# The first stage of a two-layer hybrid network: memory keys and values ahead of the input norm

## The chip, the cores and the metric

One Trainium2 chip, one core of it. The metric is the device time of one execution in microseconds (us). A core has a matrix engine (TensorE, PE in the profile, with its weight loads shown as PEld), a vector engine (VectorE, DVE), a scalar engine (ScalarE, ACT), a general engine (GpSimd, POOL) and a queue engine (SyncE, SP) that here issues every DMA. Each engine works through its own list of instructions in order; semaphores make one wait for another.

## The reference

Two layers (one "even", one "odd") on 1024 tokens of width 1024, with a memory of 256 rows. Both layers read keys and values of the same normed memory, each through its own weights.

```
mem_n = rmsnorm(mem, mem_norm_g)                       # 256 x 1024
even_layer: u = rmsnorm(h, g); za, rq, rk, rv, xq, gate = split_cols(u @ w_in, EVEN_SPLITS)
            a = pool_mixer(za, ...); r = retention(rq, rk, rv); m = mem_attention(xq, mem_n, w_mem_kv)
            h + (concat([a, r, m]) * silu(gate)) @ w_out
odd_layer:  the same frame, with a sparse attention in place of pool_mixer and retention
mem_attention: mk, mv = split(mem_n @ w_mem_kv); softmax(xq mk^T / sqrt(128)) mv, 4 heads
```

## The kernel before

Everything is kept transposed: features lie on the partitions, tokens in the free dimension, in two halves of 512 tokens. Each matrix product of full precision is made of three products: an operand is split into a rounded part (written by ACT, names ending in h) and the rest (a subtraction by DVE, names ending in l), and `mm3` (L76 to L79) multiplies h by h, h by l and l by h. So a weight tile goes DMA into `wr` (or `wm` after the change), then ACT writes `wh`, then DVE writes `wl`, then PE can use it.

The program starts with a head stage of some 64 us (pool `mk0`):

- The eight tiles `xs` of the first half of x are loaded; ACT squares each (`sqx`), and PE sums each square over the partitions by `square_sum` (L141): four products with one column for each tile, 32 in all. The memory's eight tiles are squared and summed likewise (`sqm`, two for each tile, 16 in all). Each of these fp32 products is two instructions on PE.
- From the sums comes 1/rms: `rstd_col` scales on DVE (`rs`), and POOL raises to the power -1/2 (`rr` for x, `rrkm` for the memory). `spread` makes a diagonal of it (`dg`, DVE), multiplies it by ones on PE (`ps_t<-dg,ones`), and ACT copies the row (`rb` for x, `mrb` for the memory).
- `make_u` scales the eight `xs` by `rb` on DVE (L454) and splits them into `uh` and `ul`. The first projection of the even layer, `ps_mm<-uh,wh` with the weights `ev_za`, needs them.
- `mem_kv` (L293) scales and splits the memory into `mu0` to `mu3`, makes the keys of four heads (weights `ev_mk`, products of 256 columns, 24 for each head, called K0 to K3 below) and the values (weights `ev_mv` in four quarters, 48 products of 512 columns, called V). K0 to K3 are multiplied by `mrb` into `mkx` and stored to DRAM (`evmkd`), V is scaled into `mvx` and stored (`evmvd`).

All weights go through `wr`, two buffers of 128x1024, and through four pairs `wh`, `wl`. The memory's raw tiles come through `wr` too. Behind the head stage, the even layer's two halves follow; each loads the stored keys and values (`load_mkv4`: tiles `mkr`, `mvr`) and splits them. The odd layer calls `mem_kv` a second time, between its first pairs of projections (`proj_pair`, a Strassen product with sums of weights by POOL).

The code is written in one order, and a scheduler of the language then sets each engine's order by its own estimate of when things are ready. So every change to the code can move instructions elsewhere too.

Of the kernel before, what the change touches and what calls it, by code (L numbers as in the profile page):

```python
# [9 lines left out]
F32 = mybir.dt.float32  # L10
# [29 lines left out]
def net(tc, a, out, dbg=None):  # L40
# [22 lines left out]
    def bank(tag, shape=(128, HT)):  # L63
        if tag not in banks:
            tag = ALIAS[tag]
        return cur["ps"].tile(list(shape), F32, name="ps_" + tag, tag=tag, bufs=banks[tag])
# [68 lines left out]
            pe.matmul(ss[:, t:t + 1], acc[:, t * 128:(t + 1) * 128], ones[:, 0:1], start=True, stop=True)  # L135
        return rstd_col(ss, nt, keep)

    def square_sum(ss, sq, nt, k):

        for t in range(nt):  # L140
            pe.matmul(ss[:, t:t + 1], sq[:, t * 128:(t + 1) * 128], ones[:, 0:1],  # L141
                      start=k == 0 and t == 0, stop=k == 7, skip_group_check=True)

    def rstd_col(ss, nt, keep=None):
        rs = sm.tile([128, 4], F32, name="rs")
        dve.tensor_scalar(rs[:, :nt], ss[:, :nt], 1.0 / D, EPS, OP.mult, OP.add)
# [1 line left out]
        pool.tensor_tensor(rr[:, :nt], rs[:, :nt], mhalf[:, :nt], OP.pow)  # L148
        return rr

    def spread(rr, n, raw=False, r=None):
        nt = n // 128
        rb = bank("t")
        dg = tmp.tile([128, nt, 128], F32, name="dg", tag="uf", bufs=2)
        for t in range(nt):
            dve.tensor_scalar(dg[:, t], ident, rr[:, t:t + 1], None, OP.mult)
            if raw:
                pe.matmul(rb[:, t * 128:(t + 1) * 128], ones, dg[:, t], start=True, stop=True)
        if raw:
            return rb  # L160
        pe.matmul(rb[:, :n], ones, dg.rearrange("p a b -> p (a b)"), start=True, stop=True)
        if r is None:
            r = cur["late"].tile([128, n], F32, name="rb", tag="rb")
        act.copy(r, rb[:, :n])
        return r
# [124 lines left out]

    memst = {}

    def mem_kv(pre, slots, mrb, raw=None):  # L293


        u = []
        first = not memst
        for k in range(8):
            if raw is not None:
                r = raw[k // 4]  # L300
            elif k % 4 == 0:
                r = wraw(a["memT"][k:k + 4].rearrange("k p m -> p k m"))
            x = r[:, (k % 4) * NMEM:(k % 4 + 1) * NMEM]
            s = slots[k // 2][k % 2]
            uh, ul = s[:, :NMEM], s[:, NMEM:]
            act.activation(uh, x, AF.Copy, scale=gains[:, 3, k:k + 1])
            dve.scalar_tensor_tensor(ul, x, gains[:, 3, k:k + 1], uh.bitcast(F32), OP.mult, OP.subtract)
            if first:
                if k == 0:
                    ss = bank("t")  # L310
                sq = tm2.tile([128, NMEM], F32, name="sqm", tag="th", bufs=2)
                act.activation(sq, x, AF.Square)
                square_sum(ss, sq, 2, k)
            u.append((uh, ul))
        yield
        kd = [dr.tile([128, NMEM], F32, name=f"{pre}mkd{h}") for h in range(4)]
        vd = [dr.tile([128, HT], F32, name=f"{pre}mvd{m}") for m in range(2)]
        mkv[pre] = kd, vd
        for h in range(4):
            w = wload(a[pre + "_mk"][h])  # L320
            o = bank("s")
            gemm(o[:, :NMEM], w, u)
            if first and h == 0:
                memst["rr"] = rstd_col(ss, 2, "m")
            if h == 0:
                rb = spread(memst["rr"], NMEM, r=mrb)
            t = tmp.tile([128, HT], F32, name="mkx", tag="uf", bufs=2)
            dve.tensor_tensor(t[:, :NMEM], o[:, :NMEM], rb, OP.mult)
            sp.dma_start(kd[h], t[:, :NMEM])
        yield  # L330
        o2 = [bank("s"), bank("s")]
        for c in range(4):
            w = wload(a[pre + "_mv"][c])
            for kk in range(2):
                k = 2 * c + kk
                for m in range(2):
                    mm3(o2[m], u[k][0][:, m * 128:(m + 1) * 128], u[k][1][:, m * 128:(m + 1) * 128],
                        w[kk][0], w[kk][1], k == 0, k == 7)
        for m in range(2):
            t = tmp.tile([128, HT], F32, name="mvx", tag="uf", bufs=2)  # L340
            act.activation(t, o2[m], AF.Copy, scale=memst["rr"][:, m:m + 1])
            sp.dma_start(vd[m], t)
        yield

    def load_mkv(kv, h, p_, bufs):
# [90 lines left out]
    evx = ExitStack()  # L436
    tm2 = evx.enter_context(tc.tile_pool(name="tm2", bufs=1, reuse_waits="tile"))

    def make_u(srcs, n, gi, pool_, tag, rr=None, xs=None):
        def load(k):  # L440
            x = up.tile([128, n], F32, name="x", tag="x", bufs=4)
            sp.dma_start(x, srcs[k])
            return x

        if rr is None:
            acc = tm2.tile([128, n], F32, name="acc", tag="acc")
            for k in range(8):
                add_square(acc, load(k), n, k == 0)
            rr = rstd_of(acc, n)
        rb = spread(rr, n, r=tm2.tile([128, n], F32, name="rb", tag="rb"))  # L450
        u = []
        for k in range(8):
            uf = xs[k] if xs else tmp.tile([128, n], F32, name="uf", tag="uf", bufs=2)
            dve.scalar_tensor_tensor(uf, xs[k] if xs else load(k), gains[:, gi, k:k + 1], rb, OP.mult, OP.mult)  # L454
            uh = pool_.tile([128, n], F32R, name="uh", tag=tag, bufs=16)
            ul = pool_.tile([128, n], F32R, name="ul", tag=tag, bufs=16)
            split(uh, ul, uf)
            u.append((uh, ul))
        return u

    def load_mkv4(kv, p_):
        mk = p_.tile([128, 4, 2, NMEM], F32R, name="mk", tag="mk")
        mv = p_.tile([128, 2, 2, HT], F32R, name="mv", tag="mv")
        for h in range(4):
            t = p_.tile([128, NMEM], F32, name="mkr", tag="mkx", bufs=1)
            sp.dma_start(t, kv[0][h])
            split(mk[:, h, 0], mk[:, h, 1], t)
        for m in range(2):
            t = p_.tile([128, HT], F32, name="mvr", tag="mkx", bufs=1)
            sp.dma_start(t, kv[1][m])  # L470
            split(mv[:, m, 0], mv[:, m, 1], t)
        return mk, mv
# [53 lines left out]
            pass  # L526

    sp.dma_start(ident, a["ident"])
    with tc.tile_pool(name="mk0", bufs=1, reuse_waits="tile") as mp_:
        xs = [mp_.tile([128, HT], F32, name=f"xs{k}") for k in range(8)]  # L530
        ss = bank("t")
        for k in range(8):
            sp.dma_start(xs[k], a["xT"][k][:, :HT])
            sq = tm2.tile([128, HT], F32, name="sqx", tag="t2", bufs=2)
            act.activation(sq, xs[k], AF.Square)
            square_sum(ss, sq, 4, k)
        mrb = mp_.tile([128, NMEM + 24], F32, name="mrb")[:, :NMEM]
        slots = [[mp_.tile([128, HT], F32R, name=f"mu{k}{x}") for x in "hl"] for k in range(4)]
        mem = mem_kv("ev", slots, mrb)
        u = make_u(None, HT, 0, up, "u", rstd_col(ss, 4), xs)  # L540
        drain(mem)

    rh = []
# [1 line left out]
    if True:  # L545
# [11 lines left out]
        for hf in range(2):  # L557
# [80 lines left out]
            with ExitStack() as pc:  # L638
                pp = pc.enter_context(tc.tile_pool(name="pp", bufs=1, reuse_waits="tile"))
                mp_ = pc.enter_context(tc.tile_pool(name="mx", bufs=1, reuse_waits="tile"))  # L640

                def mem_head(h):
                    s1 = gate_s1(wload(a["ev_gate"][12 + h]), u, ep)
                    o = mem_att_w(wload(a["ev_xq"][h]), u, mk, mv, h, mp_)
                    y = make_yt(ep, o, s1, 0.5)
                    ys[12 + h] = split_y(ep, y, 16)

                pooled = pool_in(0)
                mk, mv = load_mkv4(mkv["ev"], mp_)
                mem_head(0)  # L650
                pool_out(0, pooled)
                mem_head(1)
                pool_gate(0, 1, 2)
                pooled = pool_in(1)
                mem_head(2)
                pool_out(1, pooled)
                mem_head(3)
                pool_gate(3)

            with tc.tile_pool(name="rp", bufs=1, reuse_waits="tile") as rp:  # L660
# [408 lines left out]
    with tc.tile_pool(name="mk1", bufs=1, reuse_waits="tile") as mp_:  # L1069
        raw = [mp_.tile([128, 4 * NMEM], F32, name=f"mraw{j}") for j in range(2)]  # L1070
        for j in range(2):
            sp.dma_start(raw[j].rearrange("p (k m) -> p k m", k=4), a["memT"][4 * j:4 * j + 4].rearrange("k p m -> p k m"))
        mrb = mp_.tile([128, NMEM], F32, name="mrb1")
        slots = [[mp_.tile([128, HT], F32R, name=f"mv{k}{x}") for x in "hl"] for k in range(4)]
        mem = mem_kv("od", slots, mrb, raw)
        for nm, i in (("kc", 0), ("vc", 0), ("q", 0)):
            proj_pair(nm, i)
            next(mem)
    rel_tables()
    proj_pair("q", 2)  # L1080
    compress()
# [375 lines left out]
```

## Time and profile before

| | us |
|---|---|
| median of 3 runs | 2005.99 (2005.44 to 2006.42) |
| profiled execution, device time | 2006.08 |
| its span, first to last instruction | 2004.30 |
| outside the span | 1.78 |

The profiled execution is within 0.1 us of the median. Times in the trace count from the span's start. A busy PE means an instruction was in it; whether PE worked at full clock is read from the granted clock and from the pitch of its products.

### The profile page before, as it was taken

How to read it: one execution, taken by the hardware profiler on the slowest of the kernel's cores; microseconds unless marked ns; L12 is line 12 of the kernel's file. 1: busy time of each engine (PE TensorE's matmuls, PEld its weight loads, DVE VectorE, ACT ScalarE, POOL GpSimd, SP SyncE). 2: the span in 40 equal slices, each digit the busy share in tenths (PEclk: the TensorE clock that was granted, in tenths of full speed). 3: DMA queues.
4: the chain of work that ended last, by engine and by line, in shares of the span. 5: the costliest groups of instructions: out<-in, count | busy, mean ns of one | idle time of the engine just before them, and what ended most of it. 6: DMA issues, size and time to landing. Idle time of an engine off the chain costs nothing.

```text
span 2004.3 us, 28802 instructions
## 1 busy us (share of the span) xinstructions
PE 1939.9 (97%) x9898; PEld 1629.3 (81%) x9898; DVE 1269.6 (63%) x2739; ACT 941.8 (47%) x1869; POOL 572.9 (29%) x601
## 2 busy tenths in 40 slices
PE   7999999999999999999999999997999999999997
PEld 6888888888888878787878788886888888888885
DVE  4666455665646564944549855765756677867674
ACT  4545332444432243522222434544756677667674
POOL 0120110011211000314537543333343444433422
PEclk9999999999999999998999999998999999999998
DMA  5524234442322444557646433438464532251412
GB/s 164 164 83 136 90 105 137 145 159 85 93 88 95 144 152 163 166 187 221 207 143 197 137 120 130 134 101 272 149 189 127 160 104 63 69 159 42 122 32 95
DMA packets 127959, 267.07 MB, mean 133 GB/s; under 512 B 15512, under 2 KB 32676, under 8 KB 127780
## 3 DMA queue, kind: packets, MB, share of 16 engines
q1 hardware_dynamic: 127812, 265.24, 41.5%
q8 instruction: 78, 1.28, 0.3%
q14 instruction: 69, 0.56, 0.1%
HBM read 206.44 MB, written 61.09 MB: 133 GB/s over the span
## 4 chain that ended last, share of the span: by engine, by line
PE 84%; DVE 6%; DMA 4%; issue 2%; POOL 2%; ACT 1%; SPq 0%; DVEq 0%; POOLq 0%; ACTq 0%
PE ps_mm L79 13%; PE ps_mm L77 13%; PE ps_mm L78 13%; PE ps_t L120 6%; PE ps_s L77 3%; PE ps_s L78 3%; PE ps_s L79 3%; PE ps_a L77 3%; PE ps_a L78 3%; PE ps_a L79 3%; PE ps_o L84 2%; PE ps_o L82 2%; PE ps_o L83 2%; PE ps_b L79 2%; PE ps_b L78 2%
## 5 line engine op out<-in xcount | busy, mean ns | idle before, releaser
L70 ACT CAST wh<-wr 128x512 fp32r<-128x512 f32 (+1 forms) x395 | 242.4, 618 | 467.9 <-PE ps_mm L78 301.2
L71 DVE TENSOR_TENSOR wl<-wr,wh 128x512 fp32r<-128x512 f32 (+2 forms) x295 | 220.1, 750 | 178.7 <-ACT wh L70 172.2
L77 PE MATMUL ps_mm<-uh,wh 128*128 128x512 f32 x640 | 252.4, 394 | 0.0
L79 PE MATMUL ps_mm<-uh,wl 128*128 128x512 f32 x640 | 251.8, 393 | 0.0
L78 PE MATMUL ps_mm<-ul,wh 128*128 128x512 f32 x640 | 251.6, 393 | 0.0
L77 PE MATMUL ps_mm<-yh,wh 128*128 128x512 f32 x512 | 204.0, 404 | 5.1 <-ACT wh L70 3.5
L79 PE MATMUL ps_mm<-yh,wl 128*128 128x512 f32 x512 | 204.0, 400 | 2.2 <-DVE wl L71 1.4
L78 PE MATMUL ps_mm<-yl,wh 128*128 128x512 f32 x512 | 205.1, 401 | 0.0
L71 POOL TENSOR_TENSOR wl<-wr,wh 128x512 fp32r<-128x512 f32 x100 | 134.6, 1348 | 204.6 <-ACT wh L70 152.9
L71 DVE TENSOR_TENSOR apl<-ps_t,aph 128x512 fp32r<-128x512 f32 x204 | 136.1, 671 | 44.0 <-ACT aph L70 34.4
L70 ACT CAST aph<-ps_t 128x512 fp32r<-128x512 f32 x204 | 115.0, 568 | 83.0 <-PE ps_o L83 42.5
L1225 POOL TENSOR_TENSOR Pw<-Pw,arc 128x640 f32<-128x640 f32 (+2 forms) x96 | 95.9, 999 | 157.4 <-DVE arc L1221 87.8
L79 PEld LDWEIGHTS ps_mm<-uh,wl 128*128 128x128 f32 x640 | 120.2, 188 | 24.6 <-DVE wl L71 0.3
L78 PEld LDWEIGHTS ps_mm<-ul,wh 128*128 128x128 f32 x640 | 120.3, 188 | 23.8
L77 PEld LDWEIGHTS ps_mm<-uh,wh 128*128 128x128 f32 x640 | 120.3, 188 | 23.8
L77 PEld LDWEIGHTS ps_mm<-yh,wh 128*128 128x128 f32 x512 | 96.4, 190 | 26.3 <-ACT wh L70 5.9
L79 PEld LDWEIGHTS ps_mm<-yh,wl 128*128 128x128 f32 x512 | 97.1, 190 | 22.3 <-DVE wl L71 2.5
L70 ACT CAST wh<-ws 128x512 fp32r<-128x512 f32 x88 | 53.9, 619 | 129.5 <-POOL ws L231 44.3
L78 PEld LDWEIGHTS ps_mm<-yl,wh 128*128 128x128 f32 x512 | 97.3, 190 | 19.2 <-issue 0.8
L71 DVE TENSOR_TENSOR wl<-ws,wh 128x512 fp32r<-128x512 f32 x88 | 77.6, 888 | 52.2 <-ACT wh L70 49.2
L1217 ACT ACTIVATE Ps<-Ps,anm 128x512 f32<-128x512 f32 (+3 forms) x96 | 74.6, 777 | 25.8 <-DVE anm L1214 25.4
L1227 ACT ACTIVATE Ps<-Ps,arc 128x512 f32<-128x512 f32 (+3 forms) x96 | 74.7, 778 | 19.9 <-DVE arc L1221 18.8
(997 smaller groups left out, 4815.9 us busy)
## 6 DMA issues: line engine op xcount, KB each, us to landing
wr<-in_ev_gate SPq DMA_DIRECT2D x32, 512.0 KB, 3.5
wr<-in_ev_out SPq DMA_DIRECT2D x32, 512.0 KB, 3.8
wr<-in_od_out SPq DMA_DIRECT2D x64, 256.0 KB, 3.0
oa<-oho SPq DMA_DIRECT2D x52, 256.0 KB, 2.0
oxr<-oa SPq DMA_DIRECT2D x52, 256.0 KB, 2.9
wr<-in_od_q SPq DMA_DIRECT2D x16, 512.0 KB, 3.6
w<-in_cmp_w SPq DMA_DIRECT2D x16, 512.0 KB, 4.5
wr<-in_od_gate SPq DMA_DIRECT2D x16, 512.0 KB, 3.9
```

Of the source, the lines that this page charges most:

```text
L70: act.copy(hi, src)
L71: (eng or dve).tensor_tensor(lo, src, hi.bitcast(F32), OP.subtract)
L77: pe.matmul(o, wh, xh, start=start, stop=False, skip_group_check=skip)
L78: pe.matmul(o, wh, xl, start=False, stop=False, skip_group_check=skip)
L79: pe.matmul(o, wl, xh, start=False, stop=stop, skip_group_check=skip)
L82: pe.matmul(o, wh, xh, start=start, stop=False)
L83: pe.matmul(o, wl, xh, start=False, stop=False)
L84: pe.matmul(o, wh, xl, start=False, stop=stop)
L120: pe.transpose(o, x, ident[:k, :k])
L1217: act.activation(pt, pt, AF.Exp, bias=nm[:, bi:bi + 1], accum_out=su[:, bi:bi + 1])
L1225: pool.tensor_tensor(pt, pt, rc[:, bi:bi + 1].to_broadcast(list(pt.shape)), OP.mult)
L1227: act.activation(pt, pt, AF.Copy, scale=rc[:, bi:bi + 1])
```

## The change

The head stage is put in another order and gets buffers of its own. The memory comes first: the first weight tile of the keys, then the memory's eight raw tiles (`mraw`, 128 KB each), then the other weights with the x tiles between them. The eight weight tiles of keys and values have eight buffers (`wm`) and no longer share `wr`. Four of the `xs` lie in the buffers `x` in which the second half's tiles are loaded later. The squares are added up on DVE (`macc` for the memory, `xacc` for x) and summed over the partitions once: two products for the memory and four for x in place of 48. The diagonals (`dg_143`, `dg_144`) have tiles of their own. For the first half of the even layer the keys and values are split from `mkx` and `mvx` straight into tiles that stay (`mkE`), and are not read back from DRAM; they are still stored for the second half. `mem_kv` yields in other places, so that in the odd layer K0 and K1 are made behind the first pair of projections.

```diff
-    def square_sum(ss, sq, nt, k):
-
-        for t in range(nt):
-            pe.matmul(ss[:, t:t + 1], sq[:, t * 128:(t + 1) * 128], ones[:, 0:1],
-                      start=k == 0 and t == 0, stop=k == 7, skip_group_check=True)
...
-    def mem_kv(pre, slots, mrb, raw=None):
+    def mem_kv(pre, slots, mrb, raw, wsrc, macc=None, dg=None, kept=None):
...
+        r0 = wsrc(a[pre + "_mk"][0])
         for k in range(8):
...
+            for x in raw(k) if first else ():
+                sp.dma_start(x, a["memT"][k])
+        for k in range(8):
+            x = raw(k)[0]
...
-                act.activation(sq, x, AF.Square)
-                square_sum(ss, sq, 2, k)
+                add_square(macc, x, NMEM, k == 0, sq=tm2.tile([128, NMEM], F32, name="sqm", tag="th", bufs=2))
...
-                memst["rr"] = rstd_col(ss, 2, "m")
+                memst["rr"] = rstd_of(macc, NMEM, "m")
...
             sp.dma_start(kd[h], t[:, :NMEM])
+            if kept:
+                split(kept[0][:, h, 0], kept[0][:, h, 1], t[:, :NMEM])
+            if h:
+                yield
...
+        raw = [mp_.tile([128, NMEM], F32, name=f"mraw{k}") for k in range(8)]
+        macc = mp_.tile([128, NMEM], F32, name="macc")
+        dgs = [mp_.tile([128, n, 128], F32, name=f"dg{n}") for n in (2, 4)]
...
+        xs = [mp_.tile([128, HT], F32, name=f"xs{k}") for k in range(4)]
+        xs += [up.tile([128, HT], F32, name=f"xs{k}", tag="x", bufs=4) for k in range(4, 8)]
+        xacc = mp_.tile([128, HT], F32, name="xacc")
+
+        def wown(src):
+            t = mp_.tile([128, 1024], F32, name="wm", tag="wm", bufs=8)
+            sp.dma_start(t, src)
+            return t
+
+        def x_in(lo, hi):
+            for k in range(lo, hi):
+                sp.dma_start(xs[k], a["xT"][k][:, :HT])
+                add_square(xacc, xs[k], HT, k == 0, sq=tm2.tile([128, HT], F32, name="sqx", tag="t2", bufs=2))
+
+        mem = mem_kv("ev", slots, mrb, lambda k: [raw[k]], wown, macc, dgs[0], mkv0)
+        next(mem)
+        x_in(0, 4)
+        next(mem)
+        x_in(4, 8)
+        next(mem)
+        rr = rstd_of(xacc, HT)
+        u = make_u(None, HT, 0, up, "u", rr, xs, dgs[1])
         drain(mem)
...
-                mk, mv = load_mkv4(mkv["ev"], mp_)
+                mk, mv = load_mkv4(mkv["ev"], mp_) if hf else mkv0
...
-        for nm, i in (("kc", 0), ("vc", 0), ("q", 0)):
+        for (nm, i), n in ((("kc", 0), 1), (("vc", 0), 2), (("q", 0), 1)):
             proj_pair(nm, i)
-            next(mem)
+            for _ in range(n):
+                next(mem)
+        drain(mem)
```

Three places where the order of instructions is another. First SP, the DMA queue, at the program's start, before the change:

```order
L533 DMA xs_136<-in_xT 128x512
L89 DMA wr<-in_memT 128x4x256 x2
L442 DMA x<-in_xT 128x512 x5
L89 DMA wr<-in_ev_mk 128x1024 x4
L89 DMA wr<-in_ev_mv 128x1024
L329 DMA evmkd_309<-mkx 128x256
L329 DMA evmkd_310<-mkx 128x256
```

The same place of SP with the change, from the third load on (the eight `mraw` follow each other, as do the `xs` by fours):

```order
L545 DMA wm<-in_ev_mk 128x1024
L296 DMA mraw_134<-in_memT 128x256
...
L545 DMA wm<-in_ev_mk 128x1024
L550 DMA xs_154<-in_xT 128x512
...
L550 DMA xs_161<-in_xT 128x512
L545 DMA wm<-in_ev_mk 128x1024
L545 DMA wm<-in_ev_mv 128x1024 x4
L89 DMA wr<-in_ev_za 128x1024 x2
L320 DMA evmkd_212<-mkx 128x256
```

The memory and the weights stand ahead of x, the weights no longer stand behind what frees `wr`, and two loads of the first projection stand ahead of the stores. Further on, the five loads `x` of the second half stand behind those stores, and the third load of `ev_za` behind them.

Second PE at its start, before the change:

```order
L141 MATMUL ps_t<-ones,sqx 128x1 x32
L161 MATMUL ps_t<-dg,ones 128x512
L141 MATMUL ps_t<-ones,sqm 128x1 x14
L77 MATMUL ps_s<-mu0h,wh 128x256
L78 MATMUL ps_s<-mu0h,wh 128x256
L141 MATMUL ps_t<-ones,sqm 128x1 x2
```

With the change PE starts with K0 and K1, and this is what stands between K1 and K2, and then between K3 and V:

```order
L79 MATMUL ps_s<-mu3l,wl 128x256
L135 MATMUL ps_t<-ones,macc 128x1 x2
L156 MATMUL ps_t<-dg_143,ones 128x256
L135 MATMUL ps_t<-ones,xacc 128x1 x4
L77 MATMUL ps_s<-mu0h,wh 128x256
...
L156 MATMUL ps_t<-dg_144,ones 128x512
L77 MATMUL ps_s<-wh,mu0h 128x512
```

The sums moved from ahead of K0 to behind K1 and became six; the spread of x (512 columns) moved from ahead of K0 to behind K3.

Third DVE with the change, from the memory's `rs` on; first what stands between K1 and K2:

```order
L140 TENSOR_SCALAR rs<-ps_t 128x2
L129 TENSOR_TENSOR xacc<-xacc,sqx 128x512 x2
L151 TENSOR_SCALAR dg_143<-c_ident,rrkm 128x128 x2
L71 TENSOR_TENSOR wl<-wm,wh 128x512 x2
L129 TENSOR_TENSOR xacc<-xacc,sqx 128x512
L319 TENSOR_TENSOR mkx<-ps_s,mrb 128x256 x2
```

And what stands behind the eight scalings `xs_154` to `xs_161` (L453), up to the first weights of the projection:

```order
L71 TENSOR_TENSOR ul<-xs_154,uh 128x512
L71 TENSOR_TENSOR ul<-xs_155,uh 128x512
L71 TENSOR_TENSOR wl<-wm,wh 128x512
L71 TENSOR_TENSOR ul<-xs_156,uh 128x512
L71 TENSOR_TENSOR wl<-wm,wh 128x512
L71 TENSOR_TENSOR ul<-xs_157,uh 128x512
L71 TENSOR_TENSOR wl<-wm,wh 128x512
L71 TENSOR_TENSOR ul<-xs_158,uh 128x512
L71 TENSOR_TENSOR wl<-wm,wh 128x512
L71 TENSOR_TENSOR ul<-xs_159,uh 128x512
L71 TENSOR_TENSOR ul<-xs_160,uh 128x512
L71 TENSOR_TENSOR ul<-xs_161,uh 128x512
```

The eight `ul` and four of V's eight `wl` (those of its last two quarters) now stand in one row behind the scalings; before, the `ul` stood ahead of the keys' weights. Behind this stretch the orders of all engines are the same as before up to the odd layer's second call of `mem_kv`, and differ in places again in the odd layer's attention.

## Rows read from the trace of the kernel before

**Rows 1.** Windows: length, busy us (instructions) PE PEld DVE ACT POOL, PEclk, DMA share, GB/s

```profile
0.00:64.00 64.00, 50.28 (x248) 45.24 (x249) 29.80 (x60) 29.47 (x58) 4.30 (x10) 1.00 0.53 169
64.00:700.00 636.00, 636.00 (x3014) 533.76 (x3013) 377.21 (x682) 245.32 (x468) 87.74 (x69) 1.00 0.36 115
800.00:960.00 160.00, 150.67 (x725) 123.90 (x724) 98.87 (x151) 55.52 (x101) 51.74 (x39) 0.96 0.62 193
960.00:2004.30 1044.30, 1007.84 (x5498) 850.22 (x5497) 706.62 (x1750) 572.58 (x1177) 427.02 (x481) 0.98 0.41 130
```

**Rows 2.** The chain that ended last, head: start us, us, what

```profile
18.58 3.59 PE ps_t L141 x16
24.40 2.09 PE ps_t L161 x2
27.14 5.18 DVE xs L454 x8
32.44 3.09 DVE ul L71 x5
```

**Rows 3.** ACT timeline, head: start us, us, instruction, [idle before it]

```profile
5.21 1.35 ACT L535 ACTIVATE sqx<-xs 128x512 f32<-128x512 f32 x2 [3.19 <-DMA xs<-in_xT]
13.05 0.51 ACT L306 ACTIVATE mu0h<-wr,c_gains 128x256 fp32r<-128x256 f32 x1 [1.17 <-DMA wr<-in_memT]
15.80 0.49 ACT L306 ACTIVATE mu2h<-wr,c_gains 128x256 fp32r<-128x256 f32 x1
16.20 0.49 ACT L306 ACTIVATE mu2l<-wr,c_gains 128x256 fp32r<-128x256 f32 x1
26.52 0.59 ACT L164 COPY rb<-ps_t 128x512 f32<-128x512 f32 x1 [7.47 <-PE ps_t L161]
32.29 1.14 ACT L70 CAST wh<-wr 128x512 fp32r<-128x512 f32 x2 [0.45 <-DMA wr<-in_ev_mk]
```

**Rows 4.** DVE timeline, head

```profile
40.41 0.48 DVE L156 TENSOR_SCALAR dg<-c_ident,rrkm 128x128 f32<-128x128 f32 x2 [0.59 <-POOL rrkm L148]
44.83 0.75 DVE L328 TENSOR_TENSOR mkx<-ps_s,mrb 128x256 f32<-128x256 f32 x2
```

**Rows 5.** POOL timeline, head

```profile
22.43 1.01 POOL L148 TENSOR_TENSOR rr<-rs,mhalf 128x4 f32<-128x4 f32 x1 [21.49 <-DVE rs L146]
37.49 2.88 POOL L148 TENSOR_TENSOR rrkm<-rs,mhalf 128x2 f32<-128x2 f32 x1 [14.05 <-DVE rs L146]
```

**Rows 6.** PE timeline, head

```profile
36.19 0.58 PE L79 MATMUL ps_s<-mu0h,wl 128*128 128x256 f32 x1 [1.38 <-DVE wl L71]
39.77 0.41 PE L78 MATMUL ps_s<-mu2l,wh 128*128 128x256 f32 x1
39.98 0.41 PE L79 MATMUL ps_s<-mu2l,wl 128*128 128x256 f32 x1
41.14 0.28 PE L77 MATMUL ps_s<-mu0l,wh 128*128 128x256 f32 x1
41.26 0.28 PE L78 MATMUL ps_s<-mu0l,wh 128*128 128x256 f32 x1
42.58 0.59 PE L161 MATMUL ps_t<-dg,ones 128*128 128x256 f32 x2
63.30 0.39 PE L78 MATMUL ps_mm<-ul,wh 128*128 128x512 f32 x1
63.52 0.49 PE L79 MATMUL ps_mm<-uh,wl 128*128 128x512 f32 x1
```

**Rows 7.** PE timeline, odd layer's first projections

```profile
835.14 0.50 PE L77 MATMUL ps_a<-T20h,wh 128*128 128x512 f32 x1 [2.25 <-ACT wh L70]
837.29 0.63 PE L78 MATMUL ps_a<-T21l,wh 128*128 128x512 f32 x1
837.72 0.63 PE L79 MATMUL ps_a<-T21h,wl 128*128 128x512 f32 x1
```

**Rows 8.** Window of that place, columns as in the first group

```profile
837.00:838.00 1.00, 1.00 (x4) 0.81 (x3) 1.00 (x2) 1.00 (x3) 0.92 (x2) 0.50 0.79 171
```

## What the change should do to the time

> **What bounds the kernel now.** I began with the windows [rows 1]. PE is the bound: from 64 to 700 us it is busy in all 636 us, and the odd layer's first projections (800 to 960) and all that follows leave it 9.3 and 36.5 us of idle time. The head stage is different. In its 64 us PE is busy for 50.3, and much of that is poor work: the reader should see in the chain of waits [rows 2] that the sums over the partitions alone stand in it with pieces such as 16 instructions in 3.59 us (0.22 each), and that the rest of the head is one row of single steps: the memory's load to 13.05 us [rows 3], POOL's power, the spread of x (2.09 for two instructions), eight scalings on DVE (5.18), five subtractions (3.09), and only then weights and products. The first projection, which opens the saturated stretch, has its second product at 63.30 and its third, the first one that needs `wl`, at 63.52 [rows 6]. So the change is worth what it moves that third product. Between there and 700 us PE has no slack that could swallow or return anything.
>
> **The sum, step by step, in the changed kernel.** I follow the order rows of the change with durations from the rows of before.
>
> *Loads.* Before, the first x tile (0.34 MB with what is ahead of it) was usable at 5.21 and the first memory tile (2.70 MB into the queue) at 13.05 [rows 3]: 3.3 us for each MB. At that pace the first key weight (0.60 MB) lands at 6.1, the last memory tile (1.65 MB) at 9.5, the second weight (2.2) at 11.3, the third (3.75) at 16.5, the last x tile (4.8) at 20, the fourth weight (5.3) at 21.6. V's weights and the first two of the projection follow to 8.5 MB, 32 us, ahead of need. Nothing waits for `wr` any more, which is why the memory can come first.
>
> *K0 and K1.* ACT casts two weights (1.14 a pair), then scales and squares the memory at 0.40 each [rows 3]: 7.2, then 13 instructions to 12.4, then the second weight to 13.5. K0 is paced by this to about 12.5; K1 has its `wl` at about 14 and takes 24 products at 0.21 (the pitch at 39.77 and 39.98 [rows 6]), to 19. ACT meanwhile does squares and casts as they land: last memory square 18.6, `macc` 19.2 behind DVE's other work.
>
> *Between K1 and K2.* Four instructions for the memory's sum (0.9) to 20.1, `rs`, then POOL's power. It took 1.01 with DVE idle and 2.88 with DVE in subtractions [rows 5]; here DVE adds two `xacc` beside it, so I take 2.0 and keep 1.0 and 2.9. `dg` (0.48 for two [rows 4]) ends at 22.8. The fourth weight's casts end at 22.7, the last x square at 23.3, so DVE, with two `wl` and the last `xacc`, ends at 24.7. PE's sum of x, eight instructions of 0.22, ends at 26.5; `mkx` (0.75 a pair [rows 4]) is done by then and frees the bank. K2 starts at 26.5. Both chains, loads and power, end within 1 us of each other here.
>
> *K2, K3, spread.* PE has been nearly idle for some 7 us, so I let K2 start at the lower level. Before, the pitch of the key products was 0.21 up to 40.2 and 0.12 behind it [rows 6], 1.2 and 2.4 GHz for 256 columns; PE had come out of a wait at 36.19 [rows 6] and done 19 products at the lower level. I repeat that: 19 products at 0.21 and 29 at 0.12, 7.5 us, to 34.0. Bounds are 5.8 (all at 0.12) and 10.2 (all at 0.21). The spread took 2.09 at the lower level [rows 2] and 0.59 with half the columns at the higher one [rows 6]; I take 1.1. Then `rb`, 0.59 [rows 3]: 35.7.
>
> *The row on DVE.* Eight scalings, 5.18 [rows 2], to 40.9. Twelve subtractions at 0.62 (3.09 for five [rows 2]), to 48.3, and the first `wl` of the projection to 48.9. V on PE lies beside this: two quarters, 24 products at 0.23 [rows 6], from 35.1 to 40.6; then a wait of 2.2 us for the third quarter's `wl` at 42.8; then 24 products of 5.5 us to 48.3. So V ends just as DVE does. In the trace of before a wait of 2.25 us at 835.14 [rows 7] was followed by a granted clock of 0.50 [rows 8], and the products' pitch went to 0.43 [rows 7]. If that comes here, some seven products cost 0.2 more each, and V ends 1.4 later; with a longer drop, 2.0. I take 1.0 between nothing and 2.0: the third product of the projection at 49.9. That is 63.52 - 49.9 = 13.6 us earlier.
>
> *The port and the clock by the skill.* The rows on POOL show 1.01 and 2.88 us for the same operation [rows 5]. The Trainium skill ("SBUF — State Buffer", Who interferes with whom) says that a DVE instruction with two inputs in SBUF contends with a GpSimd instruction that reads SBUF, and that the one that comes second is blocked for the other's whole length; by it POOL's power would always pay for the moved squares, whose adds have two such inputs, and the sum would be 0.9 us worse at most. The rows on the clock show both levels in one stage. The Trainium skill ("TensorE: Matmul & The Clock Gate", Part 1: The HAM clock gate) makes the lower clock the state of an array that was idle, and activity what lifts it; that speaks against this change, since it takes busy instructions off PE and leaves gaps. By it alone K3 and V's second half would be slow too, some 4 us later in sum; that is rival (a) below. No row of before shows whether the new gaps do that.
>
> *Other edits.* The six reads of keys and values (`mkr`, `mvr`) leave the queue in the first half; their splits stay in number (six casts, six subtractions) and move beside K2 to V, where four of the keys' subtractions are in the sum's DVE work and two of V's fall behind the projection's start, where PE is fed ahead: nothing. The stores stay. The third `ev_za` load now stands behind four `x` loads that wait for the last `ul` (48.3) and behind V's stores; it can go out at about 52 and must have landed, cast and subtracted by 49 + 11 = 60 (two projections of 24 products at 0.23): nothing, with some 3 us in hand. In the odd layer K0 and K1 fill PE while `u` of the first pair is awaited and the second pair's weights come later; the idle time there is 9.3 us [rows 1], and I take nothing, from 2 better to 4 worse. The attention's rows are shuffled by the scheduler; its idle time is 36.5 us [rows 1], of which I allow a tenth, 3.6, either way, and take nothing.
>
> **Sum.** 2006.08 - 13.6 = 1992.5 by the profiled execution, which lies 0.1 above the median: **1992.4 us**.
>
> **Rivals.** (a) *The clock stays low.* K2, K3 and the spread at the lower level (+2.7, +1.0) and V's second half with a full drop (+1.0): 1997. For it: the 7 us with little work ahead of K2, and the wait in V. Against it: before, the clock rose inside K0, though the sums ahead of it were broken by waits. (b) *The head runs faster.* Loads at the pace reached late in the head of before and POOL alone (-1.8), all K2 and K3 at 0.12 (-1.7), the short spread (-0.5), no drop in V (-1.0): 1987.5. Each alone is likely enough, all together not. (c) *Given back later.* The odd layer's second pair is late by 4 us, since its loads stand behind two key weights in two `wr` buffers, or the attention loses a tenth more: 1996 to 2000. PE has key products to fill that hole, which speaks against it. (d) *Slower.* SP is one queue: if the third `ev_za` load, parked behind the four `x` loads and V's stores, goes out later than 56, each further us is a us of PE. From 74 on it outweighs the whole gain and the kernel is slower: at 80, 2012. Against it: what it waits for is done by 50. (e) *Nothing moves*, because the head is bound by the bytes: 8.5 MB must land before the projection, 32 us at the pace above. That is 17 us short of 49, so the pace would have to halve: 2006.
>
> **Chances and range.** Forecast (1990 to 1995) 0.58, (a) 0.15, (b) 0.12, (c) 0.10, (d) 0.02, (e) 0.03. This kernel's runs tell about 0.2%, 4 us, from no change. Faster by more than that: 0.58 + 0.15 + 0.12 + most of (c) = 0.94; within it 0.04; slower 0.02. The range reaches from (b)'s half to (a): 1988.5 to 1997.5.
>
> **What would show it.** Right: the first product with `ps_mm` near 48 to 50; K0 on PE from about 8; a gap between K1 and K2 ended by the sum of x at about 25; a wait inside V ended by `wl`; PE without idle time from the projection to where 700 us was; K2 at a pitch of 0.21 first. The forecast is wrong if K2 starts far from 26.5, if the scalings on DVE start far from 35.7, if PE waits for a load behind 50 us, or if the stretches behind the head are more than 3 us longer than before.

## The result and the profile after

The changed kernel takes 1990.7 us (median of five runs, 1987.2 to 1998.2) where the kernel before takes 2005.4 beside it (five runs): a ratio of 0.9938, 95% interval 0.9928 to 0.9949. Five more runs, taken later, gave 1992.9 against 2004.9, 0.9936 (0.9923 to 0.9948). So it is 12 to 15 us faster. The profiled execution took 1990.7 with a span of 1988.9, and its span is 15.4 shorter than that of before.

The windows answer to [rows 1] and [rows 8], with the same columns:

```profile
0.00:64.00 64.00, 49.60 (x234) 42.54 (x235) 45.10 (x92) 37.30 (x73) 6.41 (x14) 0.92 0.63 215
64.00:684.00 620.00, 620.00 (x2943) 520.48 (x2943) 365.52 (x663) 237.06 (x454) 83.05 (x65) 1.00 0.34 112
...
18.00:25.00 7.00, 3.80 (x15) 3.02 (x16) 6.21 (x16) 3.85 (x9) 1.09 (x1) 0.66 1.03 408
25.00:30.00 5.00, 5.00 (x25) 5.00 (x25) 1.63 (x6) 0.62 (x1) 1.01 (x1) 0.50 0.38 140
30.00:33.00 3.00, 3.00 (x25) 3.00 (x25) 2.05 (x4) 1.65 (x3) 0.00 (x0) 0.93 0.13 44
33.00:42.00 9.00, 7.00 (x30) 5.13 (x29) 8.67 (x16) 7.84 (x15) 0.00 (x0) 1.00 0.05 15
```

The second row is the saturated stretch, still without idle time. It lies 16 us earlier than before: PE's first wait behind the head, of 2.14 us, ends at 720.59 and not at 736.51 (PE's timelines of before, and then of the changed kernel):

```profile
736.51 0.62 PE L77 MATMUL ps_mm<-yh,wh 128*128 128x512 f32 x1 [2.14 <-ACT wh L70]
```

```profile
720.59 0.50 PE L77 MATMUL ps_mm<-yh,wh 128*128 128x512 f32 x1 [2.14 <-ACT wh L70]
```

The other rows show what was new in the head: the granted clock is down from 18 to 30 us, and up again in V.

PE's timeline of the head, beside [rows 6]:

```profile
7.15 0.58 PE L77 MATMUL ps_s<-mu0h,wh 128*128 128x256 f32 x1 [7.15 <-ACT mu0h L301]
...
18.47 0.61 PE L135 MATMUL ps_t<-ones,macc 128*128 128x1 f32 x4 [2.27 <-DVE macc L129]
21.13 1.22 PE L156 MATMUL ps_t<-dg,ones 128*128 128x256 f32 x2 [2.06 <-DVE dg L151]
23.03 1.84 PE L135 MATMUL ps_t<-ones,xacc 128*128 128x1 f32 x8 [0.68 <-DVE xacc L129]
24.73 0.56 PE L77 MATMUL ps_s<-mu0h,wh 128*128 128x256 f32 x1
25.09 0.41 PE L78 MATMUL ps_s<-mu0h,wh 128*128 128x256 f32 x1
...
30.42 0.29 PE L79 MATMUL ps_s<-mu0h,wl 128*128 128x256 f32 x1
30.55 0.28 PE L77 MATMUL ps_s<-mu0l,wh 128*128 128x256 f32 x1
...
33.07 1.02 PE L156 MATMUL ps_t<-dg,ones 128*128 128x512 f32 x2
33.52 0.80 PE L77 MATMUL ps_s<-wh,mu0h 128*128 128x512 f32 x1
...
42.04 0.50 PE L78 MATMUL ps_s<-wl,mu2h 128*128 128x512 f32 x1 [2.04 <-DVE wl L71]
42.38 0.40 PE L79 MATMUL ps_s<-wh,mu2h 128*128 128x512 f32 x1
42.62 0.39 PE L78 MATMUL ps_s<-wl,mu2h 128*128 128x512 f32 x1
...
48.07 0.49 PE L79 MATMUL ps_mm<-uh,wl 128*128 128x512 f32 x1
```

K0 starts at 7.15 in place of 32.96. Then come the gap that was forecast between K1 and K2, with three waits in it; K2 at a pitch of 0.21; 0.13 (30.42 to 30.55) from the third product of K3 on; the spread of x; V from 33.52, with a wait for `wl` inside; and the projection's third product at 48.07, which was 63.52 [rows 6]. That is 15.4 us, and the end of the program moved by as much.

The row on the other engines, beside [rows 3 to 5]:

```profile
34.12 0.59 ACT L159 COPY rb<-ps_t 128x512 f32<-128x512 f32 x1
```

```profile
22.80 0.75 DVE L319 TENSOR_TENSOR mkx<-ps_s,mrb 128x256 f32<-128x256 f32 x2
...
34.80 5.38 DVE L453 SCALAR_TENSOR_TENSOR xs<-xs,c_gains,rb 128x512 f32<-128x512 f32 x8
...
45.52 1.88 DVE L71 TENSOR_TENSOR ul<-xs,uh 128x512 fp32r<-128x512 f32 x3
47.33 1.88 DVE L71 TENSOR_TENSOR wl<-wr,wh 128x512 fp32r<-128x512 f32 x3
```

```profile
19.36 1.09 POOL L142 TENSOR_TENSOR rrkm<-rs,mhalf 128x2 f32<-128x2 f32 x1 [18.42 <-DVE rs L140]
25.14 1.01 POOL L142 TENSOR_TENSOR rr<-rs,mhalf 128x4 f32<-128x4 f32 x1 [4.70 <-DVE rs L140]
```

DVE is the engine of the last step: scalings, subtractions, the projection's first `wl`, back to back from 34.80. POOL's power for the memory took 1.09. The two `mkx` from 22.80 read the banks of K0 and K1, and K2 needs K0's bank: it was free at about 23.2, and the sum of x, which stands ahead of K2 on PE, held K2 until 24.73.

### The profile page after: what moved, and what is told of

Same layout as the page of the kernel before. It is cut to its first block, busy times and chain, and to the rows that moved or that the text cites. A ratio compares the mean times of both kernels' runs of the same rounds, so it can differ in the third digit from the quotient of the medians.

```text
span 1988.9 us, 28649 instructions
## 1 busy us (share of the span) xinstructions
PE 1920.0 (97%) x9814; PEld 1610.7 (81%) x9814; DVE 1274.1 (64%) x2753; ACT 941.9 (47%) x1869; POOL 569.0 (29%) x601
## 3 DMA queue, kind: packets, MB, share of 16 engines
q1 hardware_dynamic: 127044, 264.19, 40.1%
## 4 chain that ended last, share of the span: by engine, by line
PE 84%; DVE 5%; DMA 5%; issue 2%; POOL 2%; ACT 2%; SPq 0%; DVEq 0%; POOLq 0%; ACTq 0%
PE ps_mm L77 13%; PE ps_mm L79 13%; PE ps_mm L78 13%; PE ps_t L120 6%; PE ps_s L77 3%; PE ps_s L78 3%; PE ps_s L79 3%; PE ps_a L77 3%; PE ps_a L78 3%; PE ps_a L79 3%; PE ps_o L84 2%; PE ps_o L82 2%; PE ps_o L83 2%; PE ps_b L79 2%; PE ps_b L77 2%
## 5 line engine op out<-in xcount | busy, mean ns | idle before, releaser
L70 ACT CAST wh<-wr 128x512 fp32r<-128x512 f32 x379 | 233.4, 619 | 460.5 <-PE ps_mm L78 301.1
L71 DVE TENSOR_TENSOR wl<-wr,wh 128x512 fp32r<-128x512 f32 x279 | 208.7, 751 | 174.7 <-ACT wh L70 169.2
```

Source lines behind the costliest of these rows:

```text
L70: act.copy(hi, src)
L71: (eng or dve).tensor_tensor(lo, src, hi.bitcast(F32), OP.subtract)
```

## The experiments

Three theories stood at the start. **Theory 1**: the head is a row of single steps, and the new order shortens the row. **Theory 2**: the gain is PE's work that was taken out, 96 instructions of one column. **Theory 3**: the gain is in the weight tiles of their own. In the table "third product" is the start of the first `ps_mm` with `wl` in the profiled execution, "rest" is that execution's span behind it, and the median is that of all runs.

| kernel | third product | rest | median us (runs) | ratio to before, 95% interval |
|---|---|---|---|---|
| before | 63.5 | 1940.8 | 2005.4 (5), 2004.6 (25) | |
| own_tiles | 62.5 | 1939.5 | 2003.9 (10) | 0.9988 to 1.0007 |
| dve_sums | 57.2 | 1947.0 | 2004.0 (10) | 0.9990 to 1.0009 |
| pe_sums | 67.6 | 1940.2 | 2003.3 (10) | 0.9989 to 1.0014 |
| wr_weights | 48.6 | 1946.0 | 1993.6 (4) | 0.9935 to 0.9965 |
| changed | 48.1 | 1940.8 | 1990.7 (5) | 0.9928 to 0.9949 |
| after_again | 48.7 | 1943.6 | 1992.9 (5) | 0.9923 to 0.9948 |
| spread_early | 50.0 | 1940.2 | 1993.7 (5) | 0.9934 to 0.9959 |
| readback | 49.6 | 1942.5 | 1994.1 (5) | 0.9933 to 0.9960 |
| od_yields | 49.7 | 1944.4 | 1995.8 (5) | 0.9944 to 0.9969 |
| bank_spread | 40.0 | 1940.6 | 1981.5 (4) | 0.9868 to 0.9898 |
| bank_alone | 40.5 | 1942.9 | 1983.4 (4) | 0.9877 to 0.9905 |
| bank_again | 40.4 | 1940.3 | 1982.8 (4) | 0.9879 to 0.9906 |
| bank_od | 40.1 | 1945.5 | 1986.1 (4) | 0.9894 to 0.9921 |

**own_tiles**: the kernel before, and

```diff
+        def wown(src):
+            t = mp_.tile([128, 1024], F32, name="wm", tag="wm", bufs=8)
+            sp.dma_start(t, src)
+            return t
...
-        mem = mem_kv("ev", slots, mrb)
+        mem = mem_kv("ev", slots, mrb, None, wown)
```

> The kernel before with one part of the change alone: the eight weight tiles of keys and values lie in eight tiles of their own and no longer in wr. Theory 1 (the head is a row of single steps, and the gain comes from their new order): in the kernel before, K0 waits for a weight that itself waits for a buffer of wr, so this part shortens that one step only; the third product of the projection comes 1 to 4 us earlier than 63.52, and the kernel takes 2002 to 2005 us. Theory 3 (the tiles are what the change lives on): 10 us or more of the 15 are here, 1996 or less. Theory 2 (the gain is PE's work that was taken out): nothing, 2005.

Measured: third product 62.5, and no difference in time. The weights did land early, and K0 started at 19.79, but the list of waits on PE (us in total, times, longest) shows where the time went:

```profile
PE ps_t L161 <- DVE dg L156: 6.8, 1, 6.8
```

The memory's spread now waits 6.8 us: the memory's sum on PE stands behind K1, its `rs` on DVE behind the scalings of x (37.57), and its power on POOL, 2.88 us, beside DVE's row of subtractions. One step was shortened and another took its place. Theory 3 is out for this order.

**dve_sums**: the kernel before, and `add_square` into `macc` and `xacc` in place of `square_sum`, `rstd_of` in place of `rstd_col`.

```diff
...
-                act.activation(sq, x, AF.Square)
-                square_sum(ss, sq, 2, k)
+                add_square(macc, x, NMEM, k == 0, sq=tm2.tile([128, NMEM], F32, name="sqm", tag="th", bufs=2))
...
```

> The kernel before with another part alone: squares are added up by DVE, and PE sums them once, six products in place of 48. Theory 2: PE had 96 instructions of this kind with 21 us of busy time in the head, so most of the gain is here: 1993 to 1996. Theory 1: only the instructions that stood behind the last x tile lie in the row of steps, and DVE pays for adds in their place: the third product 1 to 4 us earlier than 63.52, 2002 to 2005. Theory 3: nothing, 2005.

Measured: third product 57.2, 6.4 us earlier, which is above the 1 to 4 of Theory 1, and yet 2004.0 us: nothing is left of it at the end. The rest of this execution is 6 us longer than before. 2 of that come in the even layer's last products, 3 in the odd layer up to the routing's products with `chid`. own_tiles shows how, since behind the third product PE has the same instructions in the same order there. The two timelines agree to 0.1 us until 735 us, and then dve_sums falls back in steps, 7.6 us in all. The first leaves it 2.5 us behind: products behind a wait go at half the pace. This is one product in own_tiles, and then in dve_sums:

```profile
746.89 0.39 PE L78 MATMUL ps_mm<-yl,wh 128*128 128x512 f32 x1
```

```profile
741.97 0.63 PE L78 MATMUL ps_mm<-yl,wh 128*128 128x512 f32 x1
```

Why the other nine runs should lose as much is not shown. PE's largest wait in the head is now for the loads of x and the adds:

```profile
PE ps_t L135 <- DVE xacc L129: 12.9, 1, 12.9
```

Theory 2 as I wrote it (1993 to 1996) is out too.

**pe_sums**: the changed kernel with the squares summed by PE again (the lines of `square_sum` and `rstd_col` put back in `mem_kv` and `x_in`).

> The changed kernel with the squares summed by PE again, 48 products (96 instructions) in place of six. Theory 2: the 21 us of PE's work are back, and most of the gain is lost: 2002 or more. Theory 1: the sums lie where PE waits anyway, and only what stands behind the last square counts, and DVE is spared the adds: the third product within 3 us of 48.07, 1988 to 1994.

Measured: 2003.3 us (2000.0 to 2011.5). The gain is gone, as Theory 2 said and against Theory 1, whose "the sums lie where PE waits anyway" was wrong. PE's timeline shows where they lie, and the windows what the clock did:

```profile
23.21 3.41 PE L140 MATMUL ps_t<-ones,sqx 128*128 128x1 f32 x16
26.48 0.56 PE L77 MATMUL ps_s<-mu0h,wh 128*128 128x256 f32 x1
...
29.62 3.41 PE L140 MATMUL ps_t<-ones,sqx 128*128 128x1 f32 x16
32.88 0.56 PE L79 MATMUL ps_s<-mu2h,wl 128*128 128x256 f32 x1
```

```profile
20.00:50.00 30.00, 27.95 (x123) 27.11 (x123) 8.59 (x22) 8.93 (x17) 2.21 (x2) 0.51 0.27 104
50.00:55.00 5.00, 5.00 (x19) 3.69 (x19) 2.29 (x4) 2.58 (x5) 0.00 (x0) 0.89 0.01 2
```

Four groups of 16 instructions for x stand ahead of and between the products of K2 and K3, 13.6 us together, and the granted clock stays at 0.51 from 20 to 50 us though PE is busy in 28 of 30. K2 and K3, with the sums among them, end at 47.1 in place of 33.1. The profiled execution took 2009.6, well above the median, so 67.6 may be more than the usual third product of this kernel.

**wr_weights**: the changed kernel with `wraw` for `wown`.

> The changed kernel with the weights of keys and values back in the two buffers of wr; memory first and all else stays. Theory 3: most of the gain is lost, 2002 or more. Theory 1: a weight can only be loaded once the one two places ahead is split, so K2, K3 and V are later by some steps of load and split: the third product at 50 to 56 and not 48.07, 1993 to 1999. Theory 2: same as the changed kernel, 1991.

Measured: 1993.6, third product 48.6. That is below the 50 to 56 that Theory 1 gave, and the same as the changed kernel, as Theory 2 had it, within what executions of one head differ by (48.1, 48.7 and, in od_yields, 49.7). In this order the weights' own tiles are worth nothing that can be seen.

So no part does it alone: the memory ahead of x (pe_sums) and the sums by DVE (dve_sums) are worth nothing singly in the time, and 11 us together (wr_weights: 1993.6 against 2004.6). With the memory first, K2 and K3 stand between the sums of x and the projection; then 64 instructions there cost what the new order gives.

**after_again**: no edit.

> The changed kernel once more, unchanged: its five times lay 11 us apart where those of the kernel before lay 3 us apart. If that spread belongs to the changed kernel, it comes again, with times near 1990 and near 1997; if it was chance, the times agree within 4 us. The trace's third product of the projection is at 48.07 within 0.5 either way.

Measured: 1988.2 to 1994.1, third product 48.7. That is neither of the two cases, and the product is 0.1 outside what was expected. The times of the kernel before lay between 2001.7 and 2008.5 in 25 runs, so its narrow first five were chance; runs of one kernel here lie 3 to 11 us apart.

**spread_early**: the changed kernel, and

```diff
...
-        next(mem)
         rr = rstd_of(xacc, HT)
-        u = make_u(None, HT, 0, up, "u", rr, xs, dgs[1])
+        rb = spread(rr, HT, r=tm2.tile([128, HT], F32, name="rb", tag="rb"), dg=dgs[1])
+        next(mem)
+        u = make_u(None, HT, 0, up, "u", rr, xs, rb)
```

> The changed kernel with the norm of x taken ahead of K3 in the code: the diagonal and the spread of x on PE stand near K3's start and not behind its end, so that the scalings on DVE can begin while K3 runs. Theory 1: the row of steps loses most of K3's length, the third product of the projection is at 44.5 to 46.5 and not 48.07, and the kernel takes 1.5 to 3.5 us less than the changed one. A rival (PE is the bound of the head behind K2, not DVE): nothing moves, or K3 and V are later by the spread's 2 us.

Measured: 1993.7, third product 50.0. The scalings did start earlier, but on DVE's timeline V's weights now stand behind them:

```profile
31.66 5.39 DVE L454 SCALAR_TENSOR_TENSOR xs<-xs,c_gains,rb 128x512 f32<-128x512 f32 x8 [0.52 <-ACT rb L159]
36.96 0.68 DVE L71 TENSOR_TENSOR wl<-wm,wh 128x512 fp32r<-128x512 f32 x1
...
39.10 4.30 DVE L71 TENSOR_TENSOR ul<-xs,uh 128x512 fp32r<-128x512 f32 x7
...
43.66 2.49 DVE L71 TENSOR_TENSOR wl<-wm,wh 128x512 fp32r<-128x512 f32 x4
```

The scalings gain 3.1 us, but two more of V's subtractions stand behind them, and its last four behind all eight `ul` instead of among them. V waits 2.82 us at 37.70, the granted clock falls behind that (0.81 from 40 to 45 us), and with the last four from 43.66 on V ends at 49.8. The rival was right: behind K2, PE has V to do, and what V needs must not be given up for x.

**bank_spread**: the edit of spread_early, and K2 and K3 in other banks. A bank is the piece of PE's accumulator memory in which a product is gathered. The group `s` has two, which K0 and K1 take; the group `mm` has three, which stand empty until the projection.

```diff
-            o = bank("s")
+            o = bank("mm" if first and h > 1 else "s")
```

> As the one with the early spread, and K2 and K3 are gathered in banks of the group mm, so that K2 need not wait until K0's bank is read by the product with mrb. Theory 1: K2 follows K1 as its weights land, without the gap from 16.2 to 24.7 but for loads, PE keeps its higher clock, and the third product is at 41 to 44: 4 to 7 us less than the changed kernel. A rival (K2 is held by its own weights, which land and are split at about 24): K2 does not start earlier, and the time is that of the early spread alone.

Measured: 1981.5 us, 11 below the changed kernel beside it, third product 40.0, which is 1 earlier than the early end of what Theory 1 gave. PE's timeline:

```profile
15.33 0.28 PE L79 MATMUL ps_s<-mu3l,wl 128*128 128x256 f32 x1
16.02 0.39 PE L77 MATMUL ps_mm<-mu0h,wh 128*128 128x256 f32 x1 [0.41 <-ACT wh L70]
...
20.06 0.39 PE L77 MATMUL ps_mm<-mu0h,wh 128*128 128x256 f32 x1
...
23.89 0.59 PE L156 MATMUL ps_t<-dg,ones 128*128 128x256 f32 x2
24.32 0.95 PE L135 MATMUL ps_t<-ones,xacc 128*128 128x1 f32 x8
25.70 0.50 PE L77 MATMUL ps_s<-wh,mu0h 128*128 128x512 f32 x1 [0.43 <-DVE mkx L319]
...
39.63 0.50 PE L78 MATMUL ps_mm<-ul,wh 128*128 128x512 f32 x1 [1.37 <-DVE ul L71]
39.96 0.39 PE L79 MATMUL ps_mm<-uh,wl 128*128 128x512 f32 x1
```

```profile
15.00:25.00 10.00, 8.69 (x67) 7.94 (x66) 9.18 (x19) 7.79 (x15) 1.08 (x1) 1.00 1.04 409
```

K2 follows K1 at 16.02 (its weight is ready then, so the rival falls), K3 at 20.06, the clock stays at 1.00, and the sums and the memory's spread find a PE that has nothing else to do. V starts at 25.70, 7.8 earlier than in the changed kernel, with its subtractions ahead of the scalings, and DVE is the bound of what is left.

**bank_alone**: only the line with the banks.

> The changed kernel with K2 and K3 gathered in banks of the group mm, and the spread of x left where the changed kernel has it in the code, behind K3. In the kernel with both edits K2 and K3 ended at 23.9, before the sum of x, so the spread would not be held by K3 any more. Theory 1a (what counted was PE's stop between K1 and K2 and the low clock behind it): the third product of the projection is within 1 us of 40.0, and the time is that of the kernel with both, 1980 to 1983. Rival (the early spread counted too): 42 or later, 1984 to 1990.

Measured: third product 40.5, 1983.4 us, as Theory 1a has it (the time 0.4 above its range); but the scheduler gave this kernel the same order on PE, DVE and ACT as the one with both edits, so it is that kernel a second time. With another bank to gather K2 in, the scheduler sets it right behind K1. The banks do it all.

**bank_again**: no edit to bank_spread.

> The kernel with both edits again, unchanged, beside the three others of this set. If it beats both kernels for good, 1979 to 1984 comes again, with the third product at 40 within 0.7.

Measured: 1982.8 (1982.0 to 1984.6), third product 40.4. With the two above, twelve runs of this order lie between 1978.9 and 1985.2, below every run of the changed kernel.

**readback**: the changed kernel without `mkE`; `load_mkv4` in both halves.

```diff
...
-                mk, mv = load_mkv4(mkv["ev"], mp_) if hf else mkv0
+                mk, mv = load_mkv4(mkv["ev"], mp_)
```

> The changed kernel with the first half's keys and values read back from DRAM and split from there again, as in the kernel before. The forecast took this part as nothing, since six loads and twelve splits lie beside a saturated PE: 1990 to 1994, the third product within 1 us of 48. A rival, that splitting at once is worth something because the third load of ev_za waits in the same queue: slower by 2 us or more. Another: the splits leave DVE's row in the head, and the third product comes 1 to 2.5 us earlier (four subtractions of 0.3 to 0.6).

Measured: 1994.1, third product 49.6: the median at the upper edge of what "nothing" allows and the product beyond it, though od_yields has the changed kernel's head and came at 49.7. The ratios of this one (0.9933 to 0.9960) and of after_again (0.9923 to 0.9948) overlap. A worth of 1 or 2 us is neither shown nor excluded.

**od_yields**: the changed kernel, with `mem_kv` yielding in the odd layer where it did before.

```diff
...
-        for (nm, i), n in ((("kc", 0), 1), (("vc", 0), 2), (("q", 0), 1)):
+        for nm, i in (("kc", 0), ("vc", 0), ("q", 0)):
             proj_pair(nm, i)
-            for _ in range(n):
-                next(mem)
+            next(mem)
```

> The changed kernel with the odd layer's call of mem_kv yielding in the old places. The head is left alone. Traces of before and after say that the odd layer's first projections gained 0.9 us and the attention lost 3.5 of which 2.4 came back later. If the yields make the 0.9, this kernel is slower by some 1 us; if they make the attention's loss too, it is faster by up to 2.5; the forecast's term was nothing, so within 1 us either way.

**bank_od**: the same edit to bank_spread.

> The kernel with both edits (K2 and K3 in banks mm, early spread), and the odd layer's yields in the old places. The changed kernel lost 3 us of its median by these old yields, at the edge of what its scatter allows. If the new yields are worth that, this kernel is 2 to 4 us above the run beside it that keeps them (1983 to 1986); if it was scatter, the two agree within 1 us.

Measured: 1995.8 against 1992.9 beside it, and 1986.1 against 1982.8. Both pairs say 3 us, more than the first of the expectations had on that side. From the odd layer's first product (`T20h`) to the routing's first (`tb`) the two took 79.9 and 79.6 us, and the kernels with the new places 76.0 to 78.5. In one wait something of it can be seen (PE's timelines of od_yields, and then of the changed kernel):

```profile
891.26 0.50 PE L77 MATMUL ps_a<-T20h,wh 128*128 128x512 f32 x1 [1.82 <-ACT wh L70]
```

```profile
887.80 0.50 PE L77 MATMUL ps_a<-T20h,wh 128*128 128x512 f32 x1 [0.71 <-ACT wh L70]
```

The third pair's weights come later. The same wait is 1.97 in bank_od, and 0.50 to 1.50 in the four other executions of the changed kernel and the bank kernels, so it is at most a part of the 3 us. And the kernel before has the old places too, and took 76.8. With the old places the rest is 1940.8 and 1939.5 us behind a late projection, and 1947.0, 1944.4 and 1945.5 behind an early one (dve_sums, od_yields, bank_od); with the new places it is 1940.2 to 1943.6, but 1946.0 in wr_weights. These are single executions, I have no mechanism for it, and why dve_sums keeps none of its 6.4 us in any run stays open.

## Why the prediction was right

1992.4 was forecast, within 1990 to 1995 for the likeliest case, and the two medians are 1990.7 and 1992.9. Its frame held for this change: the third product measures what the head gives, and the saturated stretch passes it on whole. That nothing else moves the time did not hold in general: dve_sums lost its 6.4 us behind that stretch. By its steps:

- *Loads.* The pace of 3.3 us for each MB was too slow. The fourth key weight's casts began at 19.59, where 21.6 was forecast for its landing; from 18 to 25 us the transfers ran at 408 GB/s, 2.45 us for each MB.
- *K0, K1.* K0 "from about 8" began at 7.15; K1 ended at 16.2, not 19, since it began 1.0 earlier (13.01) and the clock rose inside it.
- *Between K1 and K2.* The three waits came as forecast. POOL's power took 1.09, not 2.0, and the loads were ahead, so K2 started at 24.73 in place of 26.5. Both halves of rival (b) that were named for this place came true.
- *K2, K3, spread.* The lower level lasted for 26 products, not 19: 8.3 us in place of 7.5, a third of what rival (a) had for it. The spread took 0.45 from start to start (1.1 forecast).
- *The row on DVE.* The scalings began at 34.80 (forecast 35.7), the first `wl` at 47.33 (48.3). The row's length, 12.5 us, was right to 0.1.
- *V.* The wait inside it was 2.04 (2.2), but the pitch behind it stayed at 0.23, so the term of 1.0 for the clock was nothing. That and the earlier scalings are the 1.8 us by which 49.9 became 48.07.
- *The third `ev_za` load* went out at 52.37 ("about 52"); PE did not wait for it, and rival (d) stays a rival. Its sum is wrong: counted from the 56 that it names, the gain would be gone at 70, not 74, and 80 would give 2016, not 2012.
- *Nothing for the odd layer and the attention.* In this execution the odd layer's first projections gained 0.9, the attention lost 3.5, and 2.4 came back: within the 3.6 allowed. In medians the gain is 12 to 15 where the head moved by 15, so up to 3 us are given back in some executions. And the term for the yields was not nothing against what the same kernel would do without them: 3 us. So this nothing may be two terms that cancelled, 3 from the new yields against some 4 to 6 that are lost behind an early projection with the old ones (rest 1944.4 to 1947.0 against 1940.8, in single executions). As far as that goes, the number came out by luck.

What was weak is the reason, not the number. I called the sums "poor work" and costed their removal at the few that stood in the chain. That the new order would put all 64 of x's between K1 and V, and that the clock would stay down beside them (0.51 from 20 to 50 us in pe_sums), was not in the argument, though for this reason the new order is worth nothing without the moved sums. And the gap ahead of K2, which I forecast and let stand, was the largest cost left: it was a bank's, and one word took some 10 us off.

## What to carry to other kernels

Where an accumulator's bank waits for a scale that comes late, look for a free bank before anything else: the wait costs its own length, and the clock of the products behind it. Cost a change of order and a change of work together, since each can be worth nothing alone. And when a step is moved ahead on one engine, read on the next engine what was pushed behind it.

## What the runs showed of the hardware

**One wait, two clocks.** The first wait ahead of `T20h` in the odd layer is 2.25 or 2.26 us in all these kernels. Behind it the clock fell in some executions and not in others, with one order of instructions (PE's timelines of bank_spread, and then of bank_alone):

```profile
813.38 0.50 PE L77 MATMUL ps_a<-T20h,wh 128*128 128x512 f32 x1 [2.26 <-ACT wh L70]
...
815.10 0.63 PE L77 MATMUL ps_a<-T21h,wh 128*128 128x512 f32 x1
815.52 0.63 PE L78 MATMUL ps_a<-T21l,wh 128*128 128x512 f32 x1
```

```profile
811.37 0.50 PE L77 MATMUL ps_a<-T20h,wh 128*128 128x512 f32 x1 [2.25 <-ACT wh L70]
...
812.83 0.39 PE L77 MATMUL ps_a<-T21h,wh 128*128 128x512 f32 x1
813.06 0.39 PE L78 MATMUL ps_a<-T21l,wh 128*128 128x512 f32 x1
```

The pitch behind it is 0.42 in one and 0.23 in the other. The same holds for V's wait: 2.04 us in the changed kernel with no fall behind it, and 2.02 in od_yields, whose head has the same order on PE, with a granted clock of 0.78 from 40 to 45 us. So a term for the clock behind a wait of some 2 us is a chance, not a price. The Trainium skill ("TensorE: Matmul & The Clock Gate", Part 1: The HAM clock gate) says that one kernel shows other numbers of slow matmuls from run to run; the traces agree.

**A column that reads 1.00 need not be full speed.** In the head of before PEclk is 1.00 from the start, while products of 256 columns have a pitch of 0.21 up to 40.2 [rows 6]; the changed kernel's K0 shows the same. Ahead of the first fall the pitch tells the level, and the column does not.

**POOL beside DVE.** The power of a column took 1.01 with DVE idle. It took 2.88 in before and own_tiles, 2.28 in dve_sums and 1.20 in pe_sums, and ended 0.55 to 0.56 after the last of the subtractions that stood beside it on DVE. Beside `xacc`'s adds in the changed kernel it took 1.09, though these too have two inputs, and ended before the second of them. The Trainium skill ("SBUF — State Buffer", Who interferes with whom) calls the port pair that DVE and GpSimd share an exclusive lock, which the first comer holds for its whole instruction; the traces agree that POOL waits, and leave open why it waits for a whole row in one place and for one instruction in another.
